# A decoder layer's first stage: load order, idle products, placement of the squares and factors; the RWKV bonus product moved

## The chip, the cores and the metric

The kernel runs on one core of a Trainium2 chip. A core has a matrix engine (PE, with its weight loads shown apart as PEld), a vector engine (DVE), a scalar engine (ACT), a general-purpose engine (POOL) and an engine that only issues transfers (SP). POOL and ACT can issue transfers too. All run side by side; each works through its own instructions in order and waits on semaphores for what others produce. Matrix products go from the on-chip memory SBUF into the accumulators PSUM. The metric is the device time of one execution in microseconds (us), lower is better.

## The reference

One layer (DEPTH is 1) over 1024 positions of width 1024, in 32-bit floats:

```python
z = rmsnorm(h, norm_mix_g[l]) @ w_in[l]
a_q, a_f, a_i, a_g, b_q, b_k, b_v, c_in = jnp.split(z, splits, axis=-1)
o_a = hgrn2_mix(a_q, a_f, a_i, a_g, lbs[l], hgrn_gnorm_g[l])
o_b = dilated_window_mix(b_q, b_k, b_v)
o_c, v_first = rwkv7_mix(c_in, ...)
h = h + jnp.concatenate([o_a, o_b, o_c], axis=-1) @ w_out[l]
h = h + conv_glu_ffn(rmsnorm(h, norm_ffn_g[l]), ffn_up[l], ffn_conv_w[l], ffn_conv_b[l], ffn_down[l])
gate = jax.nn.sigmoid(rmsnorm(h, norm_ple_g[l]) @ ple_gate[l])
h = h + gate * (p[l] @ ple_proj[l])
```

The change touches the first line (norm and the first column blocks of the projection) and the RWKV-7 mixer, of which these lines matter:

```python
kk = kk / jnp.maximum(jnp.linalg.norm(kk, axis=-1, keepdims=True), 1e-12)
k = k * (1.0 + (a - 1.0) * k_a)
bonus = jnp.sum(rh * kh * r_k, axis=-1, keepdims=True) * vh
y = (y + bonus.reshape(B_, S_, RK_WIDTH)) * g
```

## The kernel before

**Layout.** The activations lie transposed: 8 row tiles k of 128 features, each in two halves (hf) of 512 positions. A projection block j is 128 columns of `w_in`; its product is an accumulator of 128 x 1024 (two PSUM banks) that sums over the 8 k. For precision every operand is split in a high part and the rest (`xh`/`xl`, `whi`/`wlo`), and each product is made of three (`mm3`, lines 137, 139, 141): high by high, high by rest, rest by high.

**The first stage** (`mix_norm`). The norm's factor depends on the position alone, so the products are formed from x times the gain, and the factor R (1 over the root of the mean square) is multiplied in later. SP's queue holds: the small parameters, then for each half one weight block of 512 KB (`raws`, blocks 0 and 1) and four x transfers of 512 KB (two row tiles each), then the constants `cst`. POOL issues two more: the back part of `par` (PC_LORA on, 256 KB) and, from `load_masks` in the RWKV preparation, the masks `ctmp` (384 KB). `split_w` makes a weight block's high part on ACT (line 114) and its rest on POOL for one half of the block and on DVE for the other (line 116). For each half and each k: ACT forms xh (L379), DVE forms xl (L380), PE makes the six products for blocks 0 and 1, ACT squares x (L384), and DVE adds the square to `acc` (L386). Behind each half, PE sums `acc` over its partitions (L183), DVE scales (L186), POOL takes the power -1/2 (L190), PE spreads the result over all partitions (L196), and ACT copies it to R (L389). Block 2 (k of the first head pair) follows for each half, in a PSUM region of its own.

**The RWKV part** (`rwkv`) goes over two head pairs p. `rwkv_prep` takes the projections k, r and v, makes the decay products on DVE (scan, reciprocals), and the operands `ar` and `bhat` of the scores (L563 to L565). `rwkv_scores` is 64 small products (L603). `rwkv_inverse` sends the scores through DRAM and inverts unit triangular 32 x 32 blocks in a long chain of dependent DVE operations (L627, L629), whose result comes back by DMA (L634, L639) for `rwkv_main` (first use L664). The bonus (L579 to L584) multiplies r, k and a parameter, sums over each head by a product with a block matrix of ones (L583), and multiplies by v. `project_rest` is a generator of further projection blocks: each `next` gives one k of a block, 6 products, and every eighth one also the block's finish on DVE and ACT. After the inverse, 8 * lead of its steps (lead 5, then 4) are issued ahead of `rwkv_main`, which draws one step per slot.

**What sets the order.** The program text is not the order on the engines. A scheduler lays the instructions of each engine in a fixed order ahead of time: among those that it believes ready, the earliest in the text comes first. Buffers are taken from pools in the same way: the projections' accumulators have two buffers (`dps`, tag `dp`), free again once DVE and ACT have read them, raw weights two (`wraw`), split weights six halves.

Of the kernel before, what the change touches and what calls it, by code (L numbers as in the profile page):

```python
# [10 lines left out]
F32 = mybir.dt.float32  # L11
F32R = mybir.dt.float32r
U8 = mybir.dt.uint8
AF = mybir.ActivationFunctionType
ALU = mybir.AluOpType
# [3 lines left out]
P = 128  # L19
T = 1024  # L20
HT = 512
ND = 8
NFF = 22
EPS = 1e-6
# [6 lines left out]
PC_W0, PC_A0, PC_KK, PC_KA, PC_RK, PC_LNW, PC_LNB = 48, 50, 52, 54, 56, 58, 60  # L31
PC_CW, PC_CB = 62, 62 + 132
PC_LORA = PC_CB + 44
# [5 lines left out]
NC0 = CC_HG = 448  # L39
# [50 lines left out]
class Trunk:  # L90
# [203 lines left out]
    def load_params(self):  # L294
        nc = self.nc
        nc.sync.dma_start(self.cst, self.a["cst"][:, :NC0])
        nc.gpsimd.dma_start(self.par[:, PC_LORA:], self.a["par"][:, PC_LORA:])
        nc.gpsimd.tensor_scalar(self.omm, self.par[:, PC_MU:PC_MU + 8], -1.0, 1.0, ALU.mult, ALU.add)

    def load_masks(self, tp):  # L300
        t = tp.tile([P, NCC - NC0], F32, name="ctmp")
        self.nc.gpsimd.dma_start(t, self.a["cst"][:, NC0:])
        self.nc.gpsimd.tensor_copy(self.cmask, t)

    def hgmask(self, l):
# [41 lines left out]
    def mix_norm(self):  # L347


        nc = self.nc  # L350
        X = self.xall()
        self.X = X
        self.R = self.keep.tile([P, T], F32, name="rstd")
        g = self.par[:, PC_MIX:PC_MIX + ND]
        halves = [slice(hf * HT, (hf + 1) * HT) for hf in (0, 1)]
        self.ps0 = ExitStack()
        ps0 = self.ps0.enter_context(self.pool("ps0", space=PSUM))
        with self.tc.tile_pool(name="st", bufs=1) as sp:
            dummy = sp.tile([P, 1], F32, name="dummy")
            nc.scalar.activation(dummy, self.ones, AF.Square)  # L360
            nc.sync.dma_start(self.par[:, :PC_LORA], self.a["par"][:, :PC_LORA])
            xs = [[sp.tile([P, 2, HT], F32, name=f"x{k}_{hf}") for k in range(4)] for hf in (0, 1)]
            xT = self.a["xT"].rearrange("(a two) p t -> a p two t", two=2)
            raws = {}
            for hf, sl in enumerate(halves):
                raws[hf] = self.wpool.tile([P, 1024], F32, tag="wraw", name=self.nm("wraw"), bufs=2)
                nc.sync.dma_start(raws[hf], self.a["w_in"][hf])
                for k in range(4):
                    nc.sync.dma_start(xs[hf][k], xT[k][:, :, sl])
            self.load_params()  # L370
            w = {j: self.split_w(raws[j]) for j in (0, 1)}
            self.early = {j: self.dps.tile([P, T], F32, tag="dp", name=self.nm("dp")) for j in (0, 1)}
            self.early[2] = ps0.tile([P, T], F32, name="dp2")
            for hf, sl in enumerate(halves):
                acc = sp.tile([P, HT], F32, tag="sacc", name=self.nm("acc"), bufs=2)
                for k in range(ND):
                    x = xs[hf][k // 2][:, k % 2, :]
                    hi, lo = X[k][0][hf], X[k][1][hf]
                    nc.scalar.activation(hi, x, AF.Copy, scale=g[:, k:k + 1])  # L379
                    nc.vector.scalar_tensor_tensor(lo, x, g[:, k:k + 1], hi.bitcast(F32), ALU.mult, ALU.subtract)  # L380
                    for j in (0, 1):
                        self.mm3({hf: self.early[j][:, sl]}, w[j](k), X[k], k == 0, k == ND - 1, (hf,))
                    t = sp.tile([P, HT], F32, tag="ssq", name=self.nm("ssq"), bufs=4) if k else acc
                    nc.scalar.activation(t, x, AF.Square)  # L384
                    if k:
                        nc.vector.tensor_tensor(acc, acc, t, ALU.add)  # L386
                pb = self.rstd_bcast(acc, 1.0 / 1024, EPS, [ps0.tile([P, n], F32, tag="n", name=self.nm("ps_ss"), bufs=2)
                                                            for n in (4, HT)])
                nc.scalar.copy(self.R[:, sl], pb)  # L389
                if hf == 0:  # L390
                    w[2] = self.load_w(self.a["w_in"][2])
                self.dense({hf: self.early[2][:, sl]}, w[2], X, ND, halves=(hf,))

    def project_rest(self, js):

# [75 lines left out]
    def rwkv(self):  # L471
        nc, tc = self.nc, self.tc
        lt = self.mix_in(0, 6, "lora")
        nc.scalar.activation(lt[0:64, :], lt[0:64, :], AF.Tanh)
        sg = self.mix_in(1, 7, "sg")
        nc.scalar.activation(sg, sg, AF.Sigmoid)
        self.z = {}
        js = iter((*range(8, 16), 24, 25, 26, 16, 17, 20, 21, 19, 27, 28, 29, 18, 22, 23))
        for p in (0, 1):
            d = {}  # L480
            with tc.tile_pool(name=f"pre{p}", bufs=1) as tp:
                self.rwkv_prep(p, tp, lt, d)
                self.rwkv_inverse(p, tp, d)
            lead, n = self.FILL[p]
            fill = self.project_rest([next(js) for _ in range(n)])
            for _ in range(8 * lead):
                next(fill)
            with tc.tile_pool(name=f"rk{p}", bufs=1) as rp:
                self.rwkv_main(p, rp, sg, d, fill)
            self.rwkv_norm(p, sg, d, 1, fill, 6 - 3 * p)  # L490
            if p == 0:
                for _ in fill:
                    pass
        self.rest, self.more = list(js), fill

    FILL = (5, 9), (4, 9)

    def rwkv_prep(self, p, tp, lt, d):

        nc, par = self.nc, self.par  # L500

        def tr(name):
            return tp.tile([P, T], F32, tag="tr", name=self.nm(name), bufs=8)

        def col(c):
            return par[:, c + p:c + p + 1]

        k = self.mix_in(2 + 3 * p, 2 + p, "k", tr)
# [4 lines left out]
        mxp = self.mxp  # L513
# [10 lines left out]
        w, a = tr("w"), tr("a")  # L524
        for hf in (0, 1):
            sl = slice(hf * HT, (hf + 1) * HT)
            ps = mxp.tile([P, HT], F32, tag="mx", name=self.nm("lo"))
            nc.tensor.matmul(ps, par[0:64, PC_LORA + p * P:PC_LORA + (p + 1) * P], lt[0:64, sl], start=True, stop=True)
            nc.scalar.activation(w[:, sl], ps, AF.Sigmoid, bias=col(PC_W0))
            ps = mxp.tile([P, HT], F32, tag="mx", name=self.nm("lo"))  # L530
# [17 lines left out]
        r = self.mix_in(3 + 3 * p, 0 + p, "r", tr)  # L548

        kkn = tr("kkn")  # L550
        for hf in (0, 1):
            sl = slice(hf * HT, (hf + 1) * HT)
            pb = mxp.tile([P, HT], F32, tag="mx", name=self.nm("kkb"))
# [10 lines left out]
        nc.vector.scalar_tensor_tensor(ar[:, 0, :, 1:], kk3[:, :, 1:], -1.0, g3[:, :, :63], ALU.mult, ALU.mult)  # L564
        nc.scalar.activation(ar[:, 0, :, 0:1], kk3[:, :, 0:1], AF.Copy, scale=-1.0)  # L565
        d.update(ar=ar, be=be, kh=kh)
        self.rwkv_scores(p, tp, d)
        v = d["v"] = self.mix_in(4 + 3 * p, 4 + p, "v")

        t = tr("ka")  # L570
# [4 lines left out]
        gC = self.spool.tile([P, 16], F32, tag="gC", name=self.nm("gC"), bufs=1)  # L575
        nc.vector.tensor_copy(gC.unsqueeze(2), g3[:, :, 63:64])
        bv = self.slot("bv")
        prod = tr("prod")
        nc.vector.scalar_tensor_tensor(prod, r, col(PC_RK), k, ALU.mult, ALU.mult)  # L579
        for hf in (0, 1):  # L580
            sl = slice(hf * HT, (hf + 1) * HT)
            pb = mxp.tile([P, HT], F32, tag="mx", name=self.nm("bon"))
            nc.tensor.matmul(pb, self.bone, prod[:, sl], start=True, stop=True)  # L583
            nc.vector.tensor_tensor(bv[:, sl], v[:, sl], pb, ALU.mult)  # L584
        d.update(bv=bv, gC=gC)

    QUADS = slice(0, 64), slice(64, 128)
    UNITS = [(u, slice(c, c + 64)) for u in range(4) for c in (0, 64)]
# [1162 lines left out]
```

## Time and profile before

| what | value |
|---|---|
| median of 3 runs | 1448.27 us (1448.19 to 1450.09) |
| the profiled execution | 1448.76 us |
| its span, first to last instruction | 1447.0 us |
| mean granted clock of PE | 0.992 |
| first product of PE | 10.30 us |
| HBM read and written over the span | 119.76 MB, 46.40 MB |

How to read the lines further on: a timeline row gives start, duration, engine, line, operation and tiles, then, in brackets, how long the engine was idle before it and what it waited for. A matmul's duration is modelled and overlaps the next; the distance of two starts is the pace. "x2" merges two. A waits row gives who waited for whom, the total, how often, and the longest. Lines such as L137 or L116 are those of helpers, which many callers share.

### The profile page before, as it was taken

Reading aid. Unit: us, or ns where it says so; the run is one execution under the profiler, and the core shown is the slowest. Engines: PE = TensorE matmul, PEld = TensorE weight load, DVE = VectorE, ACT = ScalarE, POOL = GpSimd, SP = SyncE. Lnnn points to the kernel's source line nnn. Section 1 sums busy time; section 2 is a strip of 40 time slices with the busy share of each in tenths; the row PEclk is TensorE's granted clock in tenths of the full one; section 3 lists DMA queues with packets and bytes.
Section 4 is the critical chain, followed back from the end, with each engine's and each line's share of the span. In section 5 each row is a group of like instructions: output and inputs, shape, how many; then the busy total and the mean of one; then the engine's idle time right before and its main releaser. Section 6 shows DMA issues by size and latency. Waiting matters only on the chain.

```text
span 1447.0 us, 22268 instructions
## 1 busy us (share of the span) xinstructions
PE 1398.7 (97%) x8638; PEld 1129.7 (78%) x8638; DVE 1056.1 (73%) x1617; ACT 601.6 (42%) x989; POOL 381.1 (26%) x280
## 2 busy tenths in 40 slices
PE   6999999999999999999999999999999999999996
PEld 4778777777777867787778888888888888888885
DVE  6387353863566877448878988889888799777685
ACT  6511313122244575245544444434444444455552
POOL 2311012200221332122144545545444000002332
PEclk9999999999999999999999999999999999999998
DMA  6123102230251221553322333322333973351343
GB/s 217 44 81 117 60 31 73 81 112 36 106 187 45 103 88 45 196 196 117 136 83 99 106 109 110 110 101 95 109 103 112 346 254 103 114 156 51 132 149 121
DMA packets 79674, 167.61 MB, mean 116 GB/s; under 512 B 19920, under 2 KB 22224, under 8 KB 79568
## 3 DMA queue, kind: packets, MB, share of 16 engines
q1 hardware_dynamic: 66176, 146.39, 30.2%
q10 hardware_dynamic: 12368, 15.99, 3.2%
q0 software_dynamic: 1024, 3.80, 0.7%
q8 instruction: 68, 1.11, 0.3%
q14 instruction: 38, 0.31, 0.1%
HBM read 119.76 MB, written 46.40 MB: 115 GB/s over the span
## 4 chain that ended last, share of the span: by engine, by line
PE 47%; issue 3%; DVE 2%; POOL 1%; ACT 1%; DMA 0%; POOLq 0%; ACTq 0%; DVEq 0%
PE bg L1238 16%; PE bv L1238 12%; PE bv L1532 7%; PE bg L1532 7%; PE dp L141 1%; PE dp L137 1%; PE dp L139 1%; POOL wlo L116 1%; PE bv L137 0%; PE bv L139 0%; PE bv L141 0%; ACT whi L114 0%; DVE h L1628 0%; POOL xh L162 0%; DVE gt L1627 0%
## 5 line engine op out<-in xcount | busy, mean ns | idle before, releaser
L137 PE MATMUL dp<-xh,whi 128*128 128x512 f32 x544 | 189.0, 406 | 10.5 <-ACT xh L379 10.3
L139 PE MATMUL dp<-xl,whi 128*128 128x512 f32 x544 | 183.5, 395 | 0.5 <-DVE xl L380 0.3
L141 PE MATMUL dp<-xh,wlo 128*128 128x512 f32 x544 | 183.2, 395 | 0.3 <-POOL wlo L116 0.3
L116 POOL TENSOR_TENSOR wlo<-wraw,whi 128x512 fp32r<-128x512 f32 x60 | 82.0, 1367 | 303.9 <-ACT whi L114 262.1
L116 POOL TENSOR_TENSOR wlo<-raw,whi 128x512 fp32r<-128x512 f32 x84 | 134.2, 1617 | 76.6 <-ACT whi L114 76.6
L114 ACT CAST whi<-wraw 128x512 fp32r<-128x512 f32 x120 | 73.2, 617 | 176.3 <-PE dp L139 127.3
L1238 PE MATMUL bg<-t,whi 128*128 128x512 f32 x352 | 133.2, 389 | 0.0
L137 PEld LDWEIGHTS dp<-xh,whi 128*128 128x128 f32 x544 | 99.9, 189 | 35.4 <-ACT xh L379 10.3
L139 PEld LDWEIGHTS dp<-xl,whi 128*128 128x128 f32 x544 | 102.3, 189 | 24.9 <-DVE xl L380 2.4
L141 PEld LDWEIGHTS dp<-xh,wlo 128*128 128x128 f32 x544 | 102.5, 189 | 23.3 <-issue 1.0
L116 POOL TENSOR_TENSOR wlo<-s,whi 128x512 fp32r<-128x512 f32 x44 | 64.7, 1471 | 173.6 <-ACT whi L114 173.6
L1532 PE MATMUL bg<-t,whi 128*128 128x512 f32 x308 | 95.2, 390 | 0.0
L1532 PE MATMUL bv<-t,whi 128*128 128x512 f32 x308 | 94.8, 389 | 0.0
L114 ACT CAST whi<-raw 128x512 fp32r<-128x512 f32 x88 | 52.6, 619 | 97.1 <-issue 51.5
L114 ACT CAST whi<-s 128x512 fp32r<-128x512 f32 x66 | 38.9, 620 | 121.3 <-PE bg L1238 113.5
L1238 PEld LDWEIGHTS bg<-t,whi 128*128 128x128 f32 x352 | 66.0, 188 | 13.6
L190 POOL TENSOR_TENSOR rst<-rst,mhalf 128x4 f32<-128x4 f32 (+1 forms) x9 | 10.9, 1214 | 242.3 <-DVE rst L186 225.5
L116 DVE TENSOR_TENSOR wlo<-wraw,whi 128x512 fp32r<-128x512 f32 x60 | 46.9, 782 | 30.9 <-ACT whi L114 23.9
L1532 PEld LDWEIGHTS bv<-t,whi 128*128 128x128 f32 x308 | 57.8, 188 | 12.0
L1238 PE MATMUL bg<-t,wlo 128*128 128x512 f32 x176 | 67.2, 389 | 0.0
L1532 PEld LDWEIGHTS bg<-t,whi 128*128 128x128 f32 x308 | 57.7, 188 | 11.9
L1528 ACT CAST t<-t 128x512 fp32r<-128x512 f32 x77 | 47.8, 622 | 44.9 <-PE bv L1532 29.2
(414 smaller groups left out, 3433.7 us busy)
## 6 DMA issues: line engine op xcount, KB each, us to landing
raw<-in_ffn_up_dram SPq DMA_DIRECT2D x44, 512.0 KB, 3.4
wraw<-in_w_in_dram SPq DMA_DIRECT2D x30, 512.0 KB, 3.4
z<-zst SPq DMA_DIRECT2D x18, 512.0 KB, 3.3
gb<-ct SPq DMA_DIRECT2D x33, 256.0 KB, 2.3
t<-gb SPq DMA_DIRECT2D x33, 256.0 KB, 2.7
t<-gt SPq DMA_DIRECT2D x33, 256.0 KB, 2.7
zl<-z SPq DMA_DIRECT2D x16, 512.0 KB, 3.7
wraw<-in_ple_gate_dram SPq DMA_DIRECT2D x16, 512.0 KB, 3.4
```

Source lines behind the costliest of these rows:

```text
L114: self.cast = nc.scalar.copy(hi, src).ins
L116: eng.tensor_tensor(lo, src, hi.bitcast(F32), ALU.subtract)
L137: nc.tensor.matmul(ps[hf], wh, xh[hf], start=first, stop=False)
L139: nc.tensor.matmul(ps[hf], wh, xl[hf], start=False, stop=False)
L141: nc.tensor.matmul(ps[hf], wl, xh[hf], start=False, stop=last)
L190: nc.gpsimd.tensor_tensor(r2, r, self.mhalf[:, :n], ALU.pow)
L1238: nc.tensor.matmul(ps, w[part == 2][:, s], X[k][part == 1], start=start and k == part == 0, stop=k == 3 and part == 2, skip_group_check=no ...
L1528: nc.scalar.copy(xh, x)
L1532: nc.tensor.matmul(ps[m], wt[part == 2][:, m * P:(m + 1) * P], (xh, xl)[part == 1], start=k == part == 0, stop=k == NK - 1 and part == 2)
```

## The change

In the first stage the transfers are reordered and cut: half a weight block at a time, the first half's x in order of use (some row tiles by themselves), then the second half's x; the two transfers that POOL issued move to the end of SP's queue. Two unsplit products on a zeroed tile (`idle`) are issued ahead of everything; they write block 2's accumulator, which is later started anew. In the first half no square is formed until its operands and products are through; then come its squares, with the additions on POOL. The second half keeps its squares between the products, additions on DVE. The factor of the first half is reduced at k = 5 of the second half and spread at k = 7; that of the second half is reduced ahead of block 2 and spread at block 2's k = 2. Block 2 runs over both halves at once.

In the RWKV part the generator is made ahead of `rwkv_prep`, which takes two of its steps ahead of the scores; the 8 * lead steps stay. The bonus product and its multiplication by v become `rwkv_bonus`, called behind the inverse after the fourth of those steps, and the product r k r_k is written straight into `bv`.

```diff
--- before.py
+++ after.py
@@ -294,12 +294,12 @@
     def load_params(self):
         nc = self.nc
         nc.sync.dma_start(self.cst, self.a["cst"][:, :NC0])
-        nc.gpsimd.dma_start(self.par[:, PC_LORA:], self.a["par"][:, PC_LORA:])
+        nc.sync.dma_start(self.par[:, PC_LORA:], self.a["par"][:, PC_LORA:])
         nc.gpsimd.tensor_scalar(self.omm, self.par[:, PC_MU:PC_MU + 8], -1.0, 1.0, ALU.mult, ALU.add)
 
     def load_masks(self, tp):
         t = tp.tile([P, NCC - NC0], F32, name="ctmp")
-        self.nc.gpsimd.dma_start(t, self.a["cst"][:, NC0:])
+        self.nc.sync.dma_start(t, self.a["cst"][:, NC0:])
         self.nc.gpsimd.tensor_copy(self.cmask, t)
 
     def hgmask(self, l):
@@ -361,18 +361,50 @@
             nc.sync.dma_start(self.par[:, :PC_LORA], self.a["par"][:, :PC_LORA])
             xs = [[sp.tile([P, 2, HT], F32, name=f"x{k}_{hf}") for k in range(4)] for hf in (0, 1)]
             xT = self.a["xT"].rearrange("(a two) p t -> a p two t", two=2)
-            raws = {}
-            for hf, sl in enumerate(halves):
-                raws[hf] = self.wpool.tile([P, 1024], F32, tag="wraw", name=self.nm("wraw"), bufs=2)
-                nc.sync.dma_start(raws[hf], self.a["w_in"][hf])
-                for k in range(4):
-                    nc.sync.dma_start(xs[hf][k], xT[k][:, :, sl])
+            raws = [self.wpool.tile([P, 1024], F32, tag="wraw", name=self.nm("wraw"), bufs=2) for _ in (0, 1)]
+
+            def weights(j, part):
+                c = slice(part * HT, (part + 1) * HT)
+                nc.sync.dma_start(raws[j][:, c], self.a["w_in"][j][:, c])
+
+            for k in range(4):
+                if k % 2 == 0:
+                    weights(0, k // 2)
+                    for i in (0, 1):
+                        nc.sync.dma_start(xs[0][k][:, i], xT[k][:, i, :HT])
+                    weights(1, k // 2)
+                else:
+                    nc.sync.dma_start(xs[0][k], xT[k][:, :, :HT])
+            for k in range(4):
+                nc.sync.dma_start(xs[1][k], xT[k][:, :, HT:])
             self.load_params()
-            w = {j: self.split_w(raws[j]) for j in (0, 1)}
             self.early = {j: self.dps.tile([P, T], F32, tag="dp", name=self.nm("dp")) for j in (0, 1)}
             self.early[2] = ps0.tile([P, T], F32, name="dp2")
+            idle = X[7][1][1].bitcast(F32)
+            nc.vector.memset(idle, 0.0)
+            for _ in range(2):
+                nc.tensor.matmul(self.early[2][:, :HT], idle[:, :P], idle, start=True, stop=True)
+            w = {j: self.split_w(raws[j]) for j in (0, 1)}
+
+            acc = [sp.tile([P, HT], F32, tag="sacc", name=self.nm("acc"), bufs=2) for _ in halves]
+
+            def squares(hf, k):
+                x = xs[hf][k // 2][:, k % 2, :]
+                t = sp.tile([P, HT], F32, tag="ssq", name=self.nm("ssq"), bufs=4) if k else acc[hf]
+                nc.scalar.activation(t, x, AF.Square)
+                if k:
+                    (nc.vector if hf else nc.gpsimd).tensor_tensor(acc[hf], acc[hf], t, ALU.add)
+
+            def factor(hf):
+                ps, pb = [ps0.tile([P, n], F32, tag="n", name=self.nm("ps_ss"), bufs=2) for n in (4, HT)]
+                r = self.rstd(ps, (acc[hf],))
+                yield
+                nc.scalar.copy(self.R[:, halves[hf]], self.rstd_spread(r, pb))
+                yield
+
             for hf, sl in enumerate(halves):
-                acc = sp.tile([P, HT], F32, tag="sacc", name=self.nm("acc"), bufs=2)
+                if hf:
+                    first = factor(0)
                 for k in range(ND):
                     x = xs[hf][k // 2][:, k % 2, :]
                     hi, lo = X[k][0][hf], X[k][1][hf]
@@ -380,16 +412,20 @@
                     nc.vector.scalar_tensor_tensor(lo, x, g[:, k:k + 1], hi.bitcast(F32), ALU.mult, ALU.subtract)
                     for j in (0, 1):
                         self.mm3({hf: self.early[j][:, sl]}, w[j](k), X[k], k == 0, k == ND - 1, (hf,))
-                    t = sp.tile([P, HT], F32, tag="ssq", name=self.nm("ssq"), bufs=4) if k else acc
-                    nc.scalar.activation(t, x, AF.Square)
-                    if k:
-                        nc.vector.tensor_tensor(acc, acc, t, ALU.add)
-                pb = self.rstd_bcast(acc, 1.0 / 1024, EPS, [ps0.tile([P, n], F32, tag="n", name=self.nm("ps_ss"), bufs=2)
-                                                            for n in (4, HT)])
-                nc.scalar.copy(self.R[:, sl], pb)
+                    if hf:
+                        squares(hf, k)
+                    if hf and k in (5, 7):
+                        next(first)
                 if hf == 0:
+                    for k in range(ND):
+                        squares(hf, k)
                     w[2] = self.load_w(self.a["w_in"][2])
-                self.dense({hf: self.early[2][:, sl]}, w[2], X, ND, halves=(hf,))
+            last = factor(1)
+            next(last)
+            for k in range(ND):
+                if k == 2:
+                    next(last)
+                self.mm3({i: self.early[2][:, sl] for i, sl in enumerate(halves)}, w[2](k), X[k], k == 0, k == ND - 1)
 
     def project_rest(self, js):
 
@@ -478,13 +514,15 @@
         js = iter((*range(8, 16), 24, 25, 26, 16, 17, 20, 21, 19, 27, 28, 29, 18, 22, 23))
         for p in (0, 1):
             d = {}
-            with tc.tile_pool(name=f"pre{p}", bufs=1) as tp:
-                self.rwkv_prep(p, tp, lt, d)
-                self.rwkv_inverse(p, tp, d)
             lead, n = self.FILL[p]
             fill = self.project_rest([next(js) for _ in range(n)])
-            for _ in range(8 * lead):
+            with tc.tile_pool(name=f"pre{p}", bufs=1) as tp:
+                self.rwkv_prep(p, tp, lt, d, fill)
+                self.rwkv_inverse(p, tp, d)
+            for i in range(8 * lead):
                 next(fill)
+                if i == 3:
+                    self.rwkv_bonus(d)
             with tc.tile_pool(name=f"rk{p}", bufs=1) as rp:
                 self.rwkv_main(p, rp, sg, d, fill)
             self.rwkv_norm(p, sg, d, 1, fill, 6 - 3 * p)
@@ -495,7 +533,7 @@
 
     FILL = (5, 9), (4, 9)
 
-    def rwkv_prep(self, p, tp, lt, d):
+    def rwkv_prep(self, p, tp, lt, d, fill):
 
         nc, par = self.nc, self.par
 
@@ -564,6 +602,8 @@
         nc.vector.scalar_tensor_tensor(ar[:, 0, :, 1:], kk3[:, :, 1:], -1.0, g3[:, :, :63], ALU.mult, ALU.mult)
         nc.scalar.activation(ar[:, 0, :, 0:1], kk3[:, :, 0:1], AF.Copy, scale=-1.0)
         d.update(ar=ar, be=be, kh=kh)
+        for _ in range(2):
+            next(fill)
         self.rwkv_scores(p, tp, d)
         v = d["v"] = self.mix_in(4 + 3 * p, 4 + p, "v")
 
@@ -575,14 +615,16 @@
         gC = self.spool.tile([P, 16], F32, tag="gC", name=self.nm("gC"), bufs=1)
         nc.vector.tensor_copy(gC.unsqueeze(2), g3[:, :, 63:64])
         bv = self.slot("bv")
-        prod = tr("prod")
-        nc.vector.scalar_tensor_tensor(prod, r, col(PC_RK), k, ALU.mult, ALU.mult)
+        nc.vector.scalar_tensor_tensor(bv, r, col(PC_RK), k, ALU.mult, ALU.mult)
+        d.update(bv=bv, gC=gC)
+
+    def rwkv_bonus(self, d):
+
         for hf in (0, 1):
-            sl = slice(hf * HT, (hf + 1) * HT)
-            pb = mxp.tile([P, HT], F32, tag="mx", name=self.nm("bon"))
-            nc.tensor.matmul(pb, self.bone, prod[:, sl], start=True, stop=True)
-            nc.vector.tensor_tensor(bv[:, sl], v[:, sl], pb, ALU.mult)
-        d.update(bv=bv, gC=gC)
+            b = d["bv"][:, hf * HT:(hf + 1) * HT]
+            pb = self.mxp.tile([P, HT], F32, tag="mx", name=self.nm("bon"))
+            self.nc.tensor.matmul(pb, self.bone, b, start=True, stop=True)
+            self.nc.vector.tensor_tensor(b, d["v"][:, hf * HT:(hf + 1) * HT], pb, ALU.mult)
 
     QUADS = slice(0, 64), slice(64, 128)
     UNITS = [(u, slice(c, c + 64)) for u in range(4) for c in (0, 64)]
```

## The prediction

> **What bounds the kernel now.** I read the page's busy line first, then the waits of PE over the whole span.
>
> ```profile
> PE 1398.7 (97%) x8638; PEld 1129.7 (78%) x8638; DVE 1056.1 (73%) x1617; ACT 601.6 (42%) x989; POOL 381.1 (26%) x280
> ...
> PE dp L137 <- ACT xh L379: 10.3, 1, 10.3
> PE ps_ss L196 <- POOL rst L190: 3.3, 4, 1.2
> PE sc L603 <- DVE ar L564: 2.9, 2, 1.6
> ...
> PE bon L583 <- DVE prod L579: 2.1, 2, 1.5
> ```
>
> PE is the bound: 97% busy, so a microsecond in which PE stands still early on is a microsecond at the end, as long as PE stays the bound behind it. The waits give line, releaser, total, times, longest. The largest, 10.3 us, lies ahead of the very first product. The ones on L603 and L583 (2.9 and 2.1 us, twice each, once per head pair) are the two places of the RWKV preparation that the change touches. Of L196's 3.3 us, 1.2 + 0.8 belong to the first stage (rows of 26 to 29 us and 46 to 50 us of the same view):
>
> ```profile
> PE ps_ss L196 <- POOL rst L190: 1.2, 1, 1.2
> PE ps_ss L196 <- POOL rst L190: 0.8, 1, 0.8
> ```
>
> Next, the first stage cut into stretches by what happens in them (columns: stretch, its length, PE, PEld, DVE, ACT, POOL busy with counts, granted clock, DMA share, GB/s), and two rows of its timeline that give the pace, twelve products apart.
>
> ```profile
> 10.30:15.40 5.10, 4.99 (x11) 3.04 (x11) 4.78 (x8) 5.10 (x10) 1.41 (x4) 1.00 1.04 395
> 15.40:25.10 9.70, 9.06 (x37) 6.87 (x38) 9.70 (x14) 9.70 (x18) 1.31 (x1) 1.00 0.72 264
> 25.10:32.46 7.36, 6.19 (x27) 4.96 (x26) 5.32 (x11) 4.00 (x8) 3.52 (x2) 0.77 0.15 51
> ...
> 35.15 0.39 PE L137 MATMUL dp<-xh,whi 128*128 128x512 f32 x1
> ...
> 37.87 0.39 PE L137 MATMUL dp<-xh,whi 128*128 128x512 f32 x1
> ```
>
> Undisturbed, a product takes (37.87 - 35.15) / 12 = 0.227 us. The stage has 3 blocks x 8 k x 3 parts x 2 halves = 144 of them, 32.6 us, and two reductions and spreads (L183, L196). It ends at 53.85:
>
> ```profile
> 53.62 0.39 PE L141 MATMUL dp<-xh,wlo 128*128 128x512 f32 x1
> 54.21 0.47 PE L137 MATMUL dp<-xh,whi 128*128 128x512 f32 x1 [0.20 <-DVE lora L467]
> ```
>
> What PE loses there, beside the 10.3 us: in 10.30 to 15.40 eleven products ran where 5.1 / 0.227 = 22.5 fit, 2.6 us lost (the clock column says 1.00, but the products are nearly twice as long apart as at 35 us: I read half rate from the spacing). In 15.40 to 25.10, 37 x 0.227 = 8.4 of 9.7 us: 1.3 lost to late operands. In 25.10 to 32.46 lie the 1.2 us wait and, behind it, 3.4 us at half rate (0.77 granted over 7.36 us), which lose up to 1.7, partly under the wait: I take 2.3 for both.
>
> **The change, part by part.** *Transfers.* Why is the first operand so late?
>
> ```profile
> 1.20 0.42 SPq L367 DMA_DIRECT2D wraw<-in_w_in_dram  x1
> ...
> 4.70 1.14 ACT L114 CAST whi<-wraw 128x512 fp32r<-128x512 f32 x2 [1.47 <-DMA wraw<-in_w_in_dram]
> ...
> 9.52 0.72 ACT L379 ACTIVATE xh<-x,par 128x512 fp32r<-128x512 f32 x1 [3.69 <-DMA x<-in_xT_dram]
> ...
> 10.30 0.80 PE L137 MATMUL dp<-xh,whi 128*128 128x512 f32 x1 [10.30 <-ACT xh L379]
> ...
> ctmp<-in_cst_dram POOLq DMA_DIRECT2D x1, 384.0 KB, 7.7
> par<-in_par_dram POOLq DMA_DIRECT2D x1, 256.0 KB, 4.9
> ...
> wraw<-in_w_in_dram SPq DMA_DIRECT2D x1, 512.0 KB, 3.5
> ...
> x<-in_xT_dram SPq DMA_DIRECT2D x1, 512.0 KB, 7.8
> ```
>
> par (119 KB) and the whole first weight block (512 KB) are in by 4.70; the first x, the next 512 KB, needs until 9.5, since POOL's 640 KB move beside it. In the new order the same 631 KB hold par, half of w0 and the first half of x's first pair, and POOL's two transfers stand last in SP's queue. So the first x lands at about 4.70, ACT takes 0.72, and the first product starts at 5.5: **4.8 us gained**. Bounds: by 0.9 us less if each 256 KB transfer waits for its issue (SP's took 0.42), 4.8 less if the first x again waits for all that is queued. Behind it 256 KB follow every 0.65 us (395 GB/s above), so x's last pair lands at 11.2 (4.70 + 10 x 0.65, by the bytes queued ahead) and w2, now behind cst, PC_LORA and ctmp on SP, near 20, ten us ahead of its first product. PC_LORA is first read in the RWKV preparation, ctmp's masks later still.
>
> *Idle products.* Two unsplit 128x512 products on zeros; the bonus row below shows two such at full rate in 1.96 us, so about 3.9 us at half rate, from about 1.5 to 5.4 us, ahead of all real work: they cost nothing. The memset (at most the 0.68 us of an addition of that size, below) finds DVE idle. They may lift the clock before the real products come. The rate switched 5.1 us after PE's start at 10.30; counted from 1.5 that is 6.6, so about 1.1 us of real work runs at half rate and loses 0.6; I take 0.8 (0 to 2.6, the full old loss): **1.8 gained**. The Trainium skill, "TensorE: Matmul & The Clock Gate", Part 1, says that the gate looks at free-running windows of about 3.4 us and opens after a busy one; the 3.4 us of half rate above agree. By it the switch falls anywhere between 3.4 and 6.8 us behind the start, which is inside my bounds.
>
> *First half's operands ahead of its squares.* ACT and DVE then do only operands until x's last pair is in. Supply (11.2 + 0.71 + 0.74 = 12.7 for the last) outruns 48 products (5.5 + 10.9 = 16.4). But the second weight block's low half comes by POOL (1.3 us) near 8.0, so I leave 1.0 of the 1.3 us: **0.3 gained**. The squares (8 x 0.62 on ACT) then delay the second half's first operand to about 17.6, which is just when PE gets there.
>
> *First factor inside the second half, last one inside the third block.* Between reduction and spread stand 2 k's or 12 products, 2.7 us each way, against POOL's 1.5 us (mean, row L190 below) for the power: both waits go, and with the first the half rate: 2.3 + 0.8 = **3.1 gained**. The 0.36 us between 53.85 and 54.21 go too (R is ready 7 us earlier): **0.4**.
>
> *What it adds.* Seven of the additions go to POOL. The groups of the first 60 us (count, then busy and mean ns of one), and three rows:
>
> ```profile
> L183 PE MATMUL ps_ss<-few,acc 128*128 128x1 f32 x16 | 1.9, 240 | 0.0
> L196 PE MATMUL ps_ss<-cst,rst 128*128 128x128 f32 x8 | 1.7, 354 | 2.0 <-POOL rst L190 2.0
> L384 ACT ACTIVATE ssq<-x 128x512 f32<-128x512 f32 x14 | 8.6, 616 | 0.0
> L190 POOL TENSOR_TENSOR rst<-rst,mhalf 128x4 f32<-128x4 f32 x2 | 3.0, 1524 | 8.3 <-DVE rst L186 8.3
> L386 DVE TENSOR_TENSOR acc<-acc,ssq 128x512 f32<-128x512 f32 x14 | 9.5, 678 | 0.0
> ...
> L116 POOL TENSOR_TENSOR wlo<-wraw,whi 128x512 fp32r<-128x512 f32 x6 | 7.9, 1325 | 20.4 <-ACT whi L114 20.4
> ...
> 15.85 0.74 DVE L380 SCALAR_TENSOR_TENSOR xl<-x,par,xh 128x512 fp32r<-128x512 f32 x1
> ...
> 17.03 1.31 POOL L116 TENSOR_TENSOR wlo<-wraw,whi 128x512 fp32r<-128x512 f32 x1 [5.32 <-ACT whi L114]
> 17.11 1.77 DVE L380 SCALAR_TENSOR_TENSOR xl<-x,par,xh 128x512 fp32r<-128x512 f32 x1
> ```
>
> On POOL they take 7 x 1.33 = 9.3 us, from about 13 to 23, ahead of the reduction near 25. But a DVE operand beside a POOL operation took 1.77 for 0.74: 1.03 us lost. In the second half DVE has 8 x 0.74 + 7 x 0.68 + 0.68 = 11.4 us of work in PE's 12.7 (48 products, and 1.9 / 2 + 1.7 / 2 for one reduction and spread). Three additions run before it starts; four meet it, 4 us, of which some 2 reach PE: **2.0 lost** (0 to 6.0, all seven). The Trainium skill, "SBUF — State Buffer", "Practical consequences", speaks against this part: a DVE instruction with two SBUF inputs and a GpSimd one that reads SBUF shut each other out for a whole instruction. The row agrees (1.03 us); by the rule alone it would be all seven.
>
> First stage: 4.8 + 1.8 + 0.3 + 3.1 + 0.4 - 2.0 = **8.4 us**.
>
> *Two fill steps ahead of the scores, bonus behind the inverse.*
>
> ```profile
> 80.72 1.27 DVE L467 SCALAR_TENSOR_TENSOR r<-dp,par,r 128x1023 f32<-128x1023 f32 x1
> ...
> 86.37 0.82 PE L603 MATMUL sc<-ar,bhat 64*64 64x64 f32 x41 [1.26 <-DVE ar L564]
> ...
> 94.51 1.96 PE L583 MATMUL bon<-prod,cst 128*128 128x512 f32 x4 [1.54 <-DVE prod L579]
> ...
> 131.21 0.51 SPq L634 DMA_DIRECT2D Tz<-Tb  x1
> ...
> 142.90 0.28 PE L664 MATMUL py<-Tc,sc 32*32 32x32 f32 x6
> ...
> PE py L664 <- DMA Tc<-Tz: 1.1, 1, 1.1
> ```
>
> The fill's 12 products (2.7 us) cover each wait on the scores (1.3, 1.6); the bonus product has its operand tens of us early. Both stalls may go: 5.0 us. Against it, DVE's part of the bonus (two operations of L386's size, 1.3 us) now falls into the inverse, and v's scaling with it; the first pair has slack (inverse out at 131.2, used at 142.9), the second already waits 1.1 us at py. I take **3.5** (0 to 5.0). One name less flips which of DVE and POOL forms a low part between the two pairs: no work, no sign.
>
> Sum: 1448.76 (the profiled execution: span 1447.0 and 1.8 around it) - 8.4 - 3.5 = 1436.9. The three runs' median, 1448.27, lies 0.5 lower: **1436.4**.
>
> **Rivals.** (1) *POOL's additions make DVE the bound* of the second half: all seven collide, 7.2 us; DVE needs 18.6 where PE needs 12.7, so PE loses some 6.0, and behind it only the bonus stall goes: 10.4 - 6.0 + 2.1 = 6.5 us, 1442; with py later by DVE's 1.3 us in each inverse up to 1445. For: the 1.77 row. Against: ACT's squares give POOL a start.
>
> (2) *Slower: a hole at the PSUM buffers.* Two buffers take the projections. In program order the fill's block now takes one ahead of v, and v has to wait until r's is read (80.72 + 1.27 = 81.99; second pair 261.8). If PE then has only the two steps, it stands from 70.99 + 2.7 = 73.7 to 82.0, 8.3 us, and from 252.5 + 2.7 to 261.8, 6.6; with 1.7 us of half rate behind each gap, 18.3 lost against 8.4 + 5.0 gained: **1453**. It costs more than it brings from a hole of 13.4 us in all on. It comes if the fill's other six steps aren't drawn ahead. For: the order as written, and these rows:
>
> ```profile
> 260.55 1.27 DVE L467 SCALAR_TENSOR_TENSOR r<-dp,par,r 128x1023 f32<-128x1023 f32 x1
> ...
> 70.99:86.37 15.38, 14.12 (x63) 11.14 (x61) 15.38 (x14) 2.71 (x5) 0.00 (x0) 1.00 0.10 34
> 252.50:265.50 13.00, 11.42 (x51) 9.12 (x49) 13.00 (x11) 2.48 (x4) 1.30 (x1) 1.00 0.13 42
> ```
>
> DVE is busy without a gap in both, so r can't be read sooner. Against: the order on the engines follows readiness, not the text alone (r's products at 54.21 run ahead of k's norm, which is earlier in the program), and six steps of the same block, 8.2 us, fill the hole.
>
> (3) *The shift is lost on the way.* If DVE's unbroken chain up to the scores sets the pace, the 8.4 us turn into waits there and only the bonus's 2.1 stay: 1446. Against: the chain starts from the first stage's last block (k), so it moves along.
>
> (4) *No lift by the idle products*: 1.8 us less, 1438; inside the forecast.
>
> **How the numbers follow.** Forecast (1431 to 1441): 0.62. Still faster, below 1431 (all terms at their good ends are 4.8 + 2.6 + 1.3 + 3.1 + 0.4 + 5.0 = 17.2, which is 1431.1): 0.05. Rival 1: 0.18. Rival 3: 0.08, of no difference. Rival 2: 0.07. About 0.2%, 2.9 us, is what a measurement of this kernel can tell from no change. Faster 0.62 + 0.05 + 0.18 = 0.85, same 0.08, slower 0.07. The range runs from 1430.5 to 1444.5: it takes in the forecast's and most of rival 1.
>
> **What would show it.** First real product at 5.5 us; products 0.227 apart from some 7 us on; no wait of PE on POOL's power in the first 50 us; the third block's last product near 45.5 in place of 53.85; no waits at the scores and the bonus. Wrong if the first x lands past 6 us, if xl rows of 1.7 us line up beside POOL's additions in 17 to 30 us with PE waiting for them, or if PE stands over 3 us ahead of either pair's scores.

## The result: a little slower, not faster

| | us, median (lowest to highest) | ratio to the kernel before, 95% interval |
|---|---|---|
| before | 1447.89 (1445.52 to 1450.12, 20 executions) | 1 |
| changed | 1451.74 (1447.62 to 1454.56, 20 executions) | 1.0023 [1.0014, 1.0033] |
| predicted | 1436.4 (1430.5 to 1444.5) | |

The time is above the whole range; the forecast's sign was wrong. The profiled execution of the changed kernel took 1449.42 us, 1447.6 of them span; it is one of the eight shorter ones (1447.6 to 1449.4 us, granted clock 0.990 to 0.992), and the other twelve took 1451.3 to 1454.6 us at 0.986 to 0.991, so its trace shows where PE stands, but less of the half rate than the median has.

First the busy line of the changed kernel's page, then its waits of PE (line, releaser, total, times, longest), then the two kernels' ends of the first stage.

```profile
PE 1403.9 (97%) x8642; PEld 1129.2 (78%) x8642; DVE 1062.3 (73%) x1611; ACT 600.8 (42%) x989; POOL 393.2 (27%) x285
```

```profile
PE swq L1125 <- DVE zst L460: 3.2, 1, 3.2
PE dp L137 <- DVE r L503: 2.8, 2, 1.4
...
PE dp L139 <- DVE xl L412: 2.3, 4, 1.2
PE bon L626 <- DVE bv L618: 2.1, 1, 2.1
...
PE dp L386 <- DVE few L287: 1.5, 1, 1.5
...
PE dp L137 <- DVE zst L460: 1.3, 1, 1.3
PE dp L137 <- ACT xh L411: 1.3, 2, 1.0
...
PE vt L1108 <- DMA zl<-z: 0.9, 1, 0.9
```

The 10.3 us ahead of the first product and the 2.9 at the scores are gone. In their place stand waits that the kernel before had not, or hardly: 2.8 for a projection buffer (L137 behind r's reading), 2.3 for low parts (0.3 before), 1.3 for another buffer (behind zst), and 3.2 + 0.9 at the first attention products. The bonus still waits 2.1. PE's busy time rose by 5.2 us (1398.7 to 1403.9); 3.8 of them are the idle products themselves (first row below). The timelines of the changed kernel and of the one before show how far the gain at the start was real:

```profile
1.53 3.78 PE L386 MATMUL dp<-xl 128*128 128x512 f32 x4 [1.53 <-DVE few L287]
6.33 0.80 PE L137 MATMUL dp<-xh,whi 128*128 128x512 f32 x1 [1.01 <-ACT xh L411]
...
57.00 0.69 PE L566 MATMUL lo<-lora,par 64*128 64x512 f32 x1
```

```profile
63.33 0.69 PE L528 MATMUL lo<-lora,par 64*128 64x512 f32 x1
```

The first product of the next stage (lo) starts 6.3 us earlier. At the first attention product the changed kernel is still 4.9 us ahead (403.60 against 408.5). Right there it stops (its timelines of PE and DVE, put together in order of time):

```profile
401.13 0.61 PE L141 MATMUL dp<-xh,wlo 128*128 128x512 f32 x2
402.60 1.07 PE L1108 MATMUL vt<-cst,zl 128*128 128x128 f32 x8 [0.86 <-DMA zl<-z]
403.60 0.48 PE L1125 MATMUL swq<-zl,zl 64*128 64x128 f32 x2
403.72 0.81 DVE L925 TENSOR_SCALAR zl<-zl,olb,lb 128x1024 f32<-128x1024 f32 x1 [3.72 <-DMA zl<-z]
404.01 0.45 PE L950 MATMUL hsc<-zl,hk 128*64 128x64 f32 x6
...
406.38 1.22 DVE L460 TENSOR_TENSOR zst<-dp,rstd 128x1024 f32<-128x1024 f32 x1
...
407.65 0.79 PE L1125 MATMUL swq<-zl,zl 64*128 64x128 f32 x2 [3.19 <-DVE zst L460]
```

PE has run out of projection products at 401.7. The second score product needs the buffer that zst (L460) frees; zst is queued on DVE behind L925, which waits 3.72 us for the load of zl. Behind the gap products take nearly double: 0.79 for 0.48. The stretches of 20 us of the changed kernel and of the one before (columns as in the prediction; the clock is the third last):

```profile
400.00:420.00 20.00, 15.74 (x114) 12.04 (x112) 8.22 (x19) 6.00 (x13) 5.34 (x5) 0.83 0.50 202
```

```profile
400.00:420.00 20.00, 19.79 (x145) 15.72 (x144) 12.87 (x31) 7.49 (x18) 5.55 (x5) 1.00 0.71 254
```

So 4.1 us of PE's time are lost to waits, and a mean clock of 0.83 over 20 us is 6.8 us at half rate, which loses up to 3.4 more (it begins at 406.7 us, 0.9 ahead of the wait's end, so some 3.0). That is more than the 4.9 us.

### The profile page after: what moved, and what is told of

Its sections match the earlier page's. It is cut to its first block, busy times and chain, and to the rows that moved or that the text cites. A ratio compares the mean times of both kernels' runs of the same rounds, so it can differ in the third digit from the quotient of the medians.

```text
span 1447.6 us, 22279 instructions
## 1 busy us (share of the span) xinstructions
PE 1403.9 (97%) x8642; PEld 1129.2 (78%) x8642; DVE 1062.3 (73%) x1611; ACT 600.8 (42%) x989; POOL 393.2 (27%) x285
## 4 chain that ended last, share of the span: by engine, by line
PE 47%; issue 3%; DVE 2%; POOL 1%; ACT 1%; DMA 0%; POOLq 0%; ACTq 0%; DVEq 0%
PE bg L1280 16%; PE bv L1280 12%; PE bv L1574 7%; PE bg L1574 7%; PE dp L141 1%; PE dp L137 1%; PE dp L139 1%; POOL wlo L116 1%; PE bv L137 0%; PE bv L139 0%; PE bv L141 0%; DVE h L1670 0%; POOL xh L162 0%; ACT whi L114 0%; DVE gt L1669 0%
## 5 line engine op out<-in xcount | busy, mean ns | idle before, releaser
L137 PE MATMUL dp<-xh,whi 128*128 128x512 f32 x544 | 188.5, 407 | 5.4 <-DVE r L503 2.8
L137 PEld LDWEIGHTS dp<-xh,whi 128*128 128x128 f32 x544 | 99.3, 188 | 33.1 <-issue 4.2
L190 POOL TENSOR_TENSOR rst<-rst,mhalf 128x4 f32<-128x4 f32 (+1 forms) x9 | 10.3, 1145 | 238.1 <-DVE rst L186 221.0
```

The lines of the kernel that those rows point to most:

```text
L137: nc.tensor.matmul(ps[hf], wh, xh[hf], start=first, stop=False)
L190: nc.gpsimd.tensor_tensor(r2, r, self.mhalf[:, :n], ALU.pow)
```

## The experiments

Three theories are named in the expectations. **E**: the two fill steps that the second pair now spends ahead of its scores are missing from the cover ahead of the attention. **S**: the loss is made in the preparation itself, by the projection buffers and the bonus. **F**: the z loads or a later stage set the time, whatever comes earlier. H, C and D are defined in the expectations where they come up.

The column "half rate" is the mean over the executions of span x (1 - granted clock): the time that the throttle would cost if PE were busy throughout. In the profiled executions 7.0 to 8.3 us of it lie in the last 30 us, in every kernel, so the differences between rows count, not the height. "Rest" is the mean span without it. The kernel before was run beside each group.

| kernel | us, median | ratio, 95% interval | half rate | rest |
|---|---|---|---|---|
| before | 1447.09, 1446.53, 1446.51 | 1 | 10.5 | 1435.2 |
| changed | 1451.74 | 1.0023 [1.0014, 1.0033] | 15.9 | 1433.7 |
| first_only | 1446.31 | 0.9985 [0.9976, 0.9995] | 12.6 | 1431.6 |
| rwkv_only | 1452.88 | 1.0035 [1.0024, 1.0047] | 14.7 | 1436.4 |
| cover10 | 1449.73 | 1.0017 [1.0004, 1.003] | 15.1 | 1433.2 |
| before_cover10 | 1452.36 | 1.003 [1.002, 1.0039] | 12.5 | 1437.9 |
| steps_p0 | 1444.5 | 0.998 [0.9972, 0.9989] | 11.2 | 1431.5 |
| steps_none | 1445.09 | 0.9984 [0.9975, 0.9994] | 11.9 | 1431.3 |
| first_adds_dve | 1442.02 | 0.9961 [0.9949, 0.9973] | 10.9 | 1429.0 |
| first_no_idle | 1444.44 | 0.9987 [0.9978, 0.9996] | 10.5 | 1433.1 |
| adds_dve | 1448.8 | 1.0017 [1.0004, 1.0029] | 16.5 | 1431.4 |
| dve_p0 | 1441.68 | 0.9963 [0.995, 0.9976] | 9.5 | 1430.4 |
| dve_p0_no_idle | 1442.4 | 0.9969 [0.9957, 0.998] | 10.6 | 1430.2 |
| first_dve_no_idle | 1441.69 | 0.9964 [0.9951, 0.9976] | 10.1 | 1429.9 |

### Each half of the change alone

first_only keeps the first stage's edits and puts the RWKV part back (no fill step ahead of the scores, bonus product in the preparation). rwkv_only does the reverse.

> The first stage as changed, the RWKV part (fill steps, bonus) as before. Theory E (emptied cover): the first stage's gain of 5 to 6 us reaches the end of the RWKV part, and what loses it is that two fill steps (12 products, 2.7 us) were spent ahead of the second pair's scores, so that PE runs out of projection products ahead of the attention's first product (line swq) while the z loads are still landing. Here the cover is the old one: a wait of PE at that product below 2 us, the time 3 to 6 us below before (ratio 0.996 to 0.998). Rival S (loss in the preparation: 1.4 us twice at the projection buffer, 2.1 us at the bonus): the same 4 to 6 us below before. Rival F (floor: the loads of z set when the attention starts, however early PE comes): a wait of some 5 us at the attention's first product and the time within 1.5 us of before.

> The first stage as before, the RWKV part as changed. Theory E: no early gain, but 10 to 12 products fewer ahead of the attention: a wait of 1.5 to 3 us at its first products and half rate behind it, 2 to 5 us above before. Rival S: no wait there; the stalls at the scores and the bonus only change places, 0 to 2 us above before. Rival F: as before within 1 us.

The two add up: -2.2 us (0.0015 x 1447) and +5.1 make +2.9, against +3.3 measured for both. The RWKV part, which the prediction had gaining, costs more than the first stage brings, and S, which allowed 0 to 2 us there, falls. (first_only's 2.2 us are less than the 3 to 6 that E expected; what is missing is found under the additions below.) In rwkv_only, with the first stage as before, the same wait stands at the same place, and the clock in 400 to 420 us is 0.83 again:

```profile
PE dp L137 <- DVE r L467: 3.2, 2, 1.8
PE swq L1089 <- DVE zst L424: 3.1, 1, 3.1
...
PE dp L137 <- DVE zst L424: 1.3, 1, 1.3
```

first_only has no such wait there, and clock 1.00. Nor has first_adds_dve (below), which gets to its first score product at 400.7 us, 2.9 ahead of the changed kernel. So an earlier arrival isn't what makes it: F falls for this place.

### More cover for the second pair

```diff
-    FILL = (5, 9), (4, 9)
+    FILL = (5, 9), (4, 10)
```

cover10 is the changed kernel with this edit, before_cover10 the kernel before with it.

> The changed kernel, with one more projection block in the second pair's fill (10 in place of 9), taken from those that are projected beside the attention: 48 products, 10.9 us, more ahead of the attention's first product. Theory E: no wait there, no half rate between 400 and 420 us, the FFN's first product some 5 us earlier than in the changed kernel, the time 5 to 8 us below the changed kernel and 3 to 6 below before. Rivals S and F: no difference to the changed kernel (1448 to 1453).

> Control: the kernel before, with the same tenth block in the second pair's fill. It had no wait of PE at the attention's first product, so theory E expects the time of before within 1.5 us. If it gains as much as the tenth block gains for the changed kernel, the block's place pays by itself and says nothing of the change.

In cover10 the wait for zst and the half rate at 406 us are gone, but 2.9 and 2.5 us stand later in the attention (rows of its waits), and the 5 to 8 us that E expected aren't there:

```profile
PE vt L1064 <- DVE ho L1058: 4.2, 3, 1.8
PE hsc L976 <- DVE ob L1172: 2.9, 1, 2.9
...
PE swq L1125 <- DVE sden L1132: 2.5, 1, 2.5
```

The pair of kernels says more: the tenth block costs the kernel before 4.3 us (0.003 x 1447), where E expected no difference, and gains the changed one 0.9, which is inside the intervals. Taking a block from the later stages has a price of its own, so neither kernel settles what the cover is worth; the next experiment does.

### The two steps in the first pair only, or not at all

```diff
-        for _ in range(2):
+        for _ in range(2 if p == 0 else 0):
             next(fill)
```

steps_p0 has this; steps_none leaves the two lines out and keeps the bonus where the change put it.

> The changed kernel, but the two fill steps ahead of the scores are drawn in the first pair only; the second pair keeps all its fill for the stretch ahead of the attention, as before the change. Theory E (the second pair's two steps shorten the cover ahead of the attention, and the wait there also halves the clock for 6.8 us): the wait of the first attention product for its zeroed tile (3.2 us) and the half-rate window at 406 us go, and the time falls by 3 to 6 us to 1446-1449, clock back to about .992. Theory H (the loss is in the holes of the preparation, 2 times 1.4 us for a projection buffer and 2.1 us at the bonus): no more than 1.5 us below the changed kernel's 1451.7.

> The changed kernel without any fill step ahead of the scores; the bonus product stays behind the inverse. Theory E: as with steps in the first pair only at the attention (no wait there, no window at 406 us), and the scores' old waits (1.3 and 1.6 us) come back, so 1446-1450. Theory H: the holes for a projection buffer (2 times 1.4) go too and only the bonus wait (2.1) stays, so it is 2 to 4 us below the kernel with steps in the first pair only. If moving the bonus alone costs nothing, it lies within 1.5 us of the kernel with the first stage's change alone (1446.3).

Theory E holds: 0.0043 x 1447 = 6.2 us less than the changed kernel by one number, which makes the change faster than the kernel before. By the table 4.7 of the difference in mean span are half rate and 2.2 the rest. The second score product of steps_p0 no longer waits:

```profile
403.92 1.03 PE L1108 MATMUL vt<-cst,zl 128*128 128x128 f32 x8
404.89 0.48 PE L1125 MATMUL swq<-zl,zl 64*128 64x128 f32 x2
405.30 0.45 PE L950 MATMUL hsc<-zl,hk 128*64 128x64 f32 x6
405.84 0.48 PE L1125 MATMUL swq<-zl,zl 64*128 64x128 f32 x2
```

Its first score product comes 1.3 us later than in the changed kernel, its second 1.8 earlier. The timelines show the two steps: the last product of the RWKV part (L760) starts at 387.1 us in the changed kernel and at 386.7 in steps_p0, and behind it 10 fill steps follow in the one, up to 401.7, and 12 in the other, up to 403.9. Two steps are 2.7 of the 4.1 us waited. The z load came 1.8 us later too (L925 at 403.72 against 401.91); why wasn't shown. H falls: the hole of 1.4 us and the bonus wait of 2.1 of the first pair are still in steps_p0. And steps_none, without the hole and with 1.2 us of waits at its bonus, isn't faster: its waits at the scores are back (2.8 us, twice 1.4). Both lie within 0.7 us of first_only by ratio. So in the first pair the steps bring nothing and cost nothing that can be measured; the code drains what isn't drawn by the end of that pair, which may be why. And the moved bonus brings nothing.

### Additions and idle products

```diff
-                    (nc.vector if hf else nc.gpsimd).tensor_tensor(acc[hf], acc[hf], t, ALU.add)
+                    nc.vector.tensor_tensor(acc[hf], acc[hf], t, ALU.add)
```

first_adds_dve is first_only with this edit; first_no_idle is first_only without the idle products (L385, L386).

> The first stage's change alone (1446.3 us), with the first half's seven additions of squares on DVE in place of POOL. Theory C (POOL's additions and DVE's split halve each other: 1.7 us for an instruction that takes about 0.74 alone): DVE's four split operations of 16 to 23 us fall from 6.9 to about 3 us, DVE has the additions for some 7 times 0.4-0.75 instead, and the first product of the next stage comes 0.5 to 3 us earlier than 57.4; time 1443.5-1446. Theory D (DVE is full there anyway, the additions only change engines): within 0.7 us of 57.4 and of 1446.3.

> The first stage's change alone (1446.3 us), without the two idle products (four instructions) ahead of the first real one; POOL's additions as changed. If the idle products lift the clock (half rate until 10.8 us with them): half rate lasts some 1 to 3.4 us longer, the stage ends 0.5 to 1.7 us later, 1446.8-1448. If they lift nothing that counts (DVE sets this stretch): within 0.5 us of 1446.3.

Theory C holds, by more than expected: 0.0024 x 1447 = 3.5 us. (One of first_adds_dve's six executions took 2801.91 us; the ratio and the last two columns leave it out, the 29 executions of the four kernels below show nothing like it, and its cause isn't known.) The groups of the first 60 us, first_only and then first_adds_dve (count, then busy, mean ns of one):

```profile
L412 DVE SCALAR_TENSOR_TENSOR xl<-x,par,xh 128x512 fp32r<-128x512 f32 x16 | 17.2, 1101 | 4.8 <-ACT xh L411 4.8
...
L396 POOL TENSOR_TENSOR acc<-acc,ssq 128x512 f32<-128x512 f32 x7 | 10.9, 1563 | 2.7 <-ACT ssq L394 2.3
...
L396 DVE TENSOR_TENSOR acc<-acc,ssq 128x512 f32<-128x512 f32 x7 | 6.9, 993 | 0.0
```

```profile
L412 DVE SCALAR_TENSOR_TENSOR xl<-x,par,xh 128x512 fp32r<-128x512 f32 x16 | 13.4, 854 | 4.1 <-ACT xh L411 4.1
...
L396 DVE TENSOR_TENSOR acc<-acc,ssq 128x512 f32<-128x512 f32 x14 | 10.2, 728 | 0.3
```

Seven additions given to POOL freed no DVE time: 17.2 + 6.9 = 24.1 us with POOL, 13.4 + 10.2 = 23.6 without. They only moved the loss to where PE waits. lo starts at 53.7 us in first_adds_dve, at 57.4 in first_only.

The idle products aren't worth their 1.8 us. Within the interval first_no_idle is as fast as first_only: 1.5 us more of the rest, 2.1 less at half rate. The timelines of first_only, first_no_idle and the changed kernel show where the distance of two starts falls from 0.43 to 0.23 us:

```profile
15.69 0.63 PE L137 MATMUL dp<-xh,whi 128*128 128x512 f32 x1
16.12 0.52 PE L139 MATMUL dp<-xl,whi 128*128 128x512 f32 x1
16.48 0.62 PE L141 MATMUL dp<-xh,wlo 128*128 128x512 f32 x2
16.93 0.40 PE L137 MATMUL dp<-xh,whi 128*128 128x512 f32 x1
```

```profile
11.60 0.63 PE L141 MATMUL dp<-xh,wlo 128*128 128x512 f32 x1
12.03 0.78 PE L137 MATMUL dp<-xh,whi 128*128 128x512 f32 x2
12.64 0.62 PE L139 MATMUL dp<-xl,whi 128*128 128x512 f32 x2
```

```profile
10.86 0.50 PE L139 MATMUL dp<-xl,whi 128*128 128x512 f32 x1
11.20 0.40 PE L141 MATMUL dp<-xh,wlo 128*128 128x512 f32 x1
```

Without idle products full rate came at about 12.3 us; with them it came 4 us later in one execution (16.4) and about 1.3 sooner in another (11.0). In the profile of first_adds_dve it came early, and was taken back after PE's wait of 1.58 us behind the idle products:

```profile
6.60 0.50 PE L137 MATMUL dp<-xh,whi 128*128 128x512 f32 x1 [1.58 <-ACT xh L411]
...
7.73 0.39 PE L141 MATMUL dp<-xh,wlo 128*128 128x512 f32 x1
7.96 0.57 PE L137 MATMUL dp<-xh,whi 128*128 128x512 f32 x1
8.52 0.80 PE L139 MATMUL dp<-xl,whi 128*128 128x512 f32 x1
```

### The repairs together

adds_dve is the whole change with the additions on DVE; dve_p0 also draws the steps in the first pair only; the two "no idle" kernels are dve_p0 and first_adds_dve without idle products.

> The whole change, with the first half's additions on DVE in place of POOL and nothing else altered. If the terms add (additions on POOL cost 3 to 4 us, the second pair's two steps 7 us, each by itself), it lies 3 to 4 us below the changed kernel: 1447.5-1449, with the wait of 3 us and the half-rate window at the first attention product still there. If the two losses were one (a kernel that is ahead at the first stage waits longer at the attention), less than 1.5 us below it.

> The change with both repairs: additions on DVE, and fill steps ahead of the scores in the first pair only. If the terms add: steps in the first pair only gave 2.0 us below before, the additions 3.4 more, so 1440-1442.5, ratio about 0.996. If the steps in the first pair and the bonus behind the inverse bring nothing, the same as the first stage alone with additions on DVE (ratio 0.9961) within 1 us. The old prediction's terms (1.3 for the scores' stall of the first pair, 1.5 and 0.6 for the bonus) would put it 2 to 3.4 us below that one.

> As the kernel with both repairs, but without the idle products at the start. If idle products lift the clock by what the prediction took (1.8 us): 1 to 2 us above it. If they bring no lift that lasts (their gap before the first real product starts a half-rate window instead): the same within 0.7 us, or up to 2 us below.

> First stage alone changed, additions on DVE, no idle products. Transfers in parts, late operands and the three-part third block alone: by the kernel with idle products (ratio 0.9961) 0.9955-0.9975; if the idle products were worth 1.8 us, 0.9973 or more; if the change of the RWKV part in the first pair alone gives anything, it lies above the kernel with both repairs and no idle products.

dve_p0, first_adds_dve and the two without idle products are one result within their intervals: 1441.7 to 1442.4 us, 4.5 to 5.6 us below the kernel before. So of the whole change only the transfers, the operands ahead of the squares, the two moved factors and block 2 over both halves bring a gain that can be measured (first_dve_no_idle has nothing else of it: 0.9964); they weren't taken apart. How far the squares gave way is less than the text of the program says: in the changed kernel's timeline ACT still forms four of the first half's eight squares, from 6.18 us on, ahead of that half's last two operands at 14.37.

adds_dve is the miss. Its median lies 2.9 us below the changed kernel's, just short of the 3 to 4 expected, but by the ratios only 0.9, inside the intervals. By the table the rest fell by 2.3 us, and the half rate stayed (16.5 against 15.9), where from first_only to first_adds_dve it fell too (12.6 to 10.9). Its lo starts 2.3 us earlier (54.7), its first score product only 0.8 (402.8), and the wait of 3.2 us is still there. Whether that wait takes back a part of what the additions gain stays open.

## Why the prediction was wrong, step by step

Of the 15 us between the forecast and the result, 8.6 belong to the RWKV part (it cost 5.1 us by rwkv_only, where 3.5 of gain were taken) and 6.2 to the first stage (2.2 gained by first_only, where 8.4 were taken).

**Two fill steps cover the scores: 2.9 us of the 5.0, of which 3.5 were taken.** What it covered came true: no wait on L645 is left. But the next projection waits for r to be read, 2.8 us for 2.9. This is the hole of rival 2 at a fifth of its price (1.4 each, not 8.3 and 6.6), because the six other steps fill it, as the text said. What failed is a sentence that isn't there: the prediction never asked where the 12 products of the second pair were missing. It named what each step covers, not what it had covered before. The place was the end of the second pair, 140 us later, at 6.2 us. That rival 2's time, 1453, lies near the measured one is luck: it got there by holes of 14.9 us at the projection buffers, and they were 2.8.

**Bonus behind the inverse: the other 2.1 us.** Nothing. In the program it moved; on PE it did not get behind the wait. The changed kernel's timeline has it 14.2 us behind the scores (79.7) in place of 8.1, but its operand was put off as well (rows of PE, then of DVE):

```profile
93.86 1.95 PE L626 MATMUL bon<-bv,cst 128*128 128x512 f32 x4 [2.07 <-DVE bv L618]
...
275.52 1.88 PE L626 MATMUL bon<-bv,cst 128*128 128x512 f32 x4
```

```profile
88.43 1.23 DVE L319 TENSOR_TENSOR dp<-dp,rstd 128x1024 f32<-128x1024 f32 x1 [3.85 <-PE dp L141]
91.83 0.70 DVE L319 TENSOR_TENSOR dp<-dp,rstd 128x512 f32<-128x512 f32 x1 [2.17 <-PE dp L141]
92.44 1.27 DVE L618 SCALAR_TENSOR_TENSOR bv<-r,par,k 128x1024 f32<-128x1024 f32 x1
```

"The bonus product has its operand tens of us early" was wrong. Both inputs of bv were there at 80.6 us (k, L612, ends last), but in DVE's fixed order bv stands behind the scaling of two projections (L319), for which DVE itself stood idle 3.85 and 2.17 us. Moving the product in the program didn't move its operand forward there. The second pair's bonus waits no more, but 1.5 us ahead of it PE waits 1.3 us for zst's buffer.

**First product, +4.8.** It came at 6.33 us, not 5.5: x was there at 5.55, not 4.70, the first bound named. And the base was too high: the other two profiles with the old first stage start at 9.35 and 9.51 us, not 10.30, which leaves 3.0 to 3.2 of the 4.8 against this execution's 6.33.

**Idle products, +1.8.** Zero within the interval (above). The Trainium skill, "TensorE: Matmul & The Clock Gate", Part 1, has the gate fall back after an idle window of about 3.4 us, free-running; the traces agree with the length (ahead of the last 30 us of the kernels, half rate lasted 3.4 or 6.8 us at a time) but show it behind gaps of 1.2 us (the kernel before, at 28.7 us) and 1.6 us (first_adds_dve, above) too. The prediction counted the rate's rise and not that the pause behind the idle products could take it back.

**Factors moved, +3.1.** The waits on POOL's power fell from 2.0 to 0.6 us. The half rate behind the first, though, belonged to one execution: rwkv_only's profile, with the same old wait, has it not (clock 1.00; the prediction's row of the same stretch has 0.77):

```profile
25.10:32.46 7.36, 6.21 (x31) 4.91 (x31) 5.73 (x11) 4.39 (x8) 3.53 (x2) 1.00 0.21 71
```

In the two other profiles with the old first stage lo starts at 60.9 and 61.5, not 63.3. So about 2 us of the 8.4 could be won only in the profiled execution that the prediction was read from.

**Additions on POOL, -2.0.** They cost 3.5, inside the bound of 6. Rival 1 was right in its mechanism (its time, 1442, isn't borne out, since it had the RWKV part gaining), and its signature of xl rows of 1.7 us came as written (DVE's timeline of the changed kernel):

```profile
16.04 6.90 DVE L412 SCALAR_TENSOR_TENSOR xl<-x,par,xh 128x512 fp32r<-128x512 f32 x4
22.87 1.77 DVE L396 TENSOR_TENSOR acc<-acc,ssq 128x512 f32<-128x512 f32 x1
24.56 0.74 DVE L412 SCALAR_TENSOR_TENSOR xl<-x,par,xh 128x512 fp32r<-128x512 f32 x1
```

Four operations in 6.90 us, 1.73 each, where the last row has 0.74 alone. Here the rule of the Trainium skill, "SBUF — State Buffer", "Practical consequences", that one of the two engines blocks for a whole instruction, was the better guide than the discount to four collisions.

**The shift is kept to the end.** For the rest it is: first_only's 3.6 us (1435.2 to 1431.6) match lo's 3.5 to 4.1. The throttle takes 2.1 back (10.5 to 12.6): in these traces a wait of PE can be followed by 3.4 us at half rate, and the prediction had priced the throttle only where the old profile showed it.

## What to carry to other kernels

Fill work is a stock. When steps of it are drawn earlier, find the place where the last of them used to run and ask what PE does there instead; here 12 products of 0.23 us (2.7 us), gone from one place, cost 6.2, more than half of it in clock by the table. Work given from DVE to POOL is free only if DVE's own durations stay as they were: add up the busy time of both forms. Before pricing a stall from one profile, look at whether it is in a second one.

## What the chip showed beyond expectation

At one place, waits of PE of 3.7 to 4.1 us cost some 2.5 to 3.1 us more in clock. All three profiled kernels with the wait at the attention's second score product (changed, rwkv_only, adds_dve) had 6.8 us at half rate there, which began in the last 0.5 to 1.8 us of that wait, at 406.3 to 407.2 us; none of the others had any between 400 and 420. The length of a wait doesn't decide it, though: in cover10 a wait of 2.90 us that ends at 511.9 has no half rate behind it, and one of 2.47 that ends at 539.4 has 6.8 us. Which waits are followed by half rate in a given execution was not shown.
